# A two-block network in one program: the routing's order and the places of weights and tokens in SBUF

## The chip, the cores and the metric

One core of a Trainium2 chip runs the whole program. The metric is the device time of one execution in microseconds. TensorE is PE in the profile, its weight loads PEld, VectorE is DVE, ScalarE is ACT, GpSimd is POOL, and SP issues most of the transfers from memory.

## The reference

All is float32, for 256 tokens of 1024 features, one batch. Shortened:

```python
# first block
h = rms_norm(x, norm1_g);  proj = h @ w_in
y = gates[0] * conformer_conv(...) + gates[1] * mla(...)      # 31-tap conv; attention with 8 heads
x = x + y @ w_out
x = x + (silu(conv3(h2 @ w_up)[gate]) * conv3(h2 @ w_up)[up]) @ w_down      # D_FF = 2816
x = rms_norm(x, norm_f_g)
# second block
x = x + pool_conv_mixer(rmsnorm(x))
x = x + swiglu(rmsnorm(x), gate, up, down)                    # D_FF = 2816
x = x + sliding_window_attention(rmsnorm(x)) @ w_o + b_o      # 16 heads, 2 of keys
h = rmsnorm(x, od_norm_ffn)
top_vals, top_idx = top_k(h @ w_router, 2)                    # 8 experts
x = x + sum(combine[e] * ((silu(h @ w_gate[e]) * (h @ w_up[e])) @ w_down[e]))   # 1024 x 3584 each
return rmsnorm(x, final_norm)
```

## The kernel before

**The dense stage.** Everything ahead of the experts keeps the tokens as columns: a tile holds two blocks of 128 features by 256 tokens ("pair", 2048 bytes in each of 128 partitions). For accuracy each weight chunk and each token tile is split into two parts in the format fp32r, a high and a low one: ACT copies the chunk's high part (`whi`), DVE subtracts it (`wlo`). `mm3` multiplies high by high, high by low and low by high: three products of 256 columns, each with a weight load of 128 x 128. Token tiles have names such as xnh/xnl (normed tokens), hh/hl (hidden), xqh/xql, oh/ol. Weights arrive as chunks of up to 1 MB (`raw`); SP issues them in the order of use, as far ahead as there are buffers.

**The routing** stands at the end of `odd`, in the last of four steps over the attention's output projection. Its rows' names are: `gw` the router's weights, `lg`/`l` the logits, `acc` and `sq` the sums of squares for the norm, `rs` its reciprocal root, `sel` the selection of two experts, `place` a token's place in its expert, `S` the matrix that gathers tokens, `xe` the gathered tokens. Steps marked `high_priority` are ordered by a scheduler that may move instructions on each engine; inside `manual_schedule` an engine's instructions stand as written. Before the change the SP queue stands as written throughout, and PE from the experts on.

**The experts.** `gate`, `up` and `down_stage` stream 352 MB of expert weights. Here the weights are the moving operand and the gathered tokens (64 columns of them at a time) are loaded. Buffers for these weights are taken over from pools that the dense stage gives up (`more0` to `more6`, and `extra0` to `extra2` where whi and wlo were).

**Where tiles lie.** Pools are laid out one after another from the low end of SBUF (`cp`, `rawp`, `sm`, `pp`, `bp`, ...), those with `side="right"` from the high end (`whip`, `wlop`, later `extra`, `ep`, `xp`). In the built program, counted from the last multiple of 512 bytes, the buffers of `rawp` start at 384, those of `pp` and `bp` (token tiles) at 128, those of whi and wlo at 480, the `more` pools at 128.

**Warm-up products** are products of constants that nobody reads: `warm(n)` makes n of 128 x 128 x 128; `warm_forms` makes some at the program's start, while the first transfers are under way. The last lines of the dense step and of the warm-up are:

```python
self.mm(ps[:, f], hi[:, cs], xh, first and k == 0 and f == 0, False)
self.mm(ps[:, f], hi[:, cs], xl, False, False)
self.mm(ps[:, f], lo[:, cs], xh, False, last and k == kn - 1)
```

A plain fp32 product has two records of each kind in the trace, an fp32r product one.

Of the kernel before, what the change touches and what calls it, by code (L numbers as in the profile page):

```python
# [34 lines left out]
NSIDE = 32  # L35
NCAP = NMAIN + NSIDE
LCAP = 128
WARM = (25, 8, 0)
FIRST_PARTS = 4
ORDER = (0, 1, 3, 4, 2, 5, 6)  # L40
N_BRIEF = 22
# [18 lines left out]
N_MM = 5  # L60
N_RAW = 6
N_PAIR = 22

# [306 lines left out]
class Body:  # L370
# [61 lines left out]
    def warm_forms(self):  # L432

        nc = self.nc
        c = self.pair("const", F32, (128, 512))
        nc.vector.memset(c, 1.0)
        self.warm(8)
        banks = [self.bank((128, 512)) for _ in range(2)]
        for n in range(2):
            self.mm(banks[n // 2 % 2][64 * (n % 2):64 * (n % 2) + 64], c[:, 64 * (n % 2):64 * (n % 2) + 64], c, True, True)  # L440
        for n in range(8):
            q = slice(32 * (n % 4), 32 * (n % 4) + 32)
            self.mm(banks[n // 4 % 2][q], c[:, q], c, True, True)

    def next(self, kn):
        self.w = self.st.next(kn)
# [92 lines left out]
    def body(self):  # L539
        tc, nc, ctx, a = self.tc, self.nc, self.ctx, self.a  # L540
        pool = lambda n, b, **kw: ctx.enter_context(tc.tile_pool(name=n, bufs=b, **kw))
        self.cp = pool("cp", 1)
        self.raw = pool("rawp", N_RAW)
        self.split = ExitStack()
        self.whi, self.wlo = (self.split.enter_context(tc.tile_pool(name=n, bufs=b, side="right"))
                              for n, b in (("whip", N_HI), ("wlop", N_LO)))
        self.sm, self.pp = pool("sm", 8), pool("pp", N_PAIR)
# [79 lines left out]

    def block1(self):
        nc = self.nc
        u = self.wp.tile([128, 4, 286], F32, name="wide")  # L630
# [17 lines left out]
        lat, lp, sq = self.act("lat", 6), self.parts("lat", 6), self.act("lsq", 6)  # L648
        kr, t = self.pair("kr"), self.pair("krt")
# [371 lines left out]
    def odd(self):  # L1021
# [38 lines left out]
        with self.tc.issue_after(self.last_sink.ins):  # L1060
# [2 lines left out]
        self.bp = None  # L1063
        self.rp = self.ctx.enter_context(self.tc.tile_pool(name="rows", bufs=N_ROW, reuse_waits="tile"))
        self.brief = ExitStack()
        more = [self.brief.enter_context(self.tc.tile_pool(name=f"more{i}", bufs=1, reuse_waits="tile"))
                for i in range(len(ORDER))]
        self.st.ring = deque([more[i] for i in ORDER] + [self.raw] * N_RAW)
# [5 lines left out]
                                self.iota[:, :NE, None].to_broadcast([128, NE, NE]), op=ALU.is_lt)  # L1074
        lg = self.aux((128, 2, 8))
        self.ex, self.S = {}, {}
        for j in range(4):
            ps = self.dense(o)
            with self.tc.high_priority(offset=HASTE):
                x = self.x.p[j]  # L1080
                for f in range(2):
                    nc.vector.scalar_tensor_tensor(x[:, f], ps[:, f], self.par("od_b_o_2", 2 * j + f), x[:, f],
                                                   op0=ALU.add, op1=ALU.add)
                for f in range(2):
                    for b in range(2):
                        self.mm(lg[:, b], x[:, f, 128 * b:128 * b + 128], gw[:, 2 * j + f], j + f + b == 0, j + f == 4)
                ps = self.aux()
                for f in range(2):
                    for b in range(2):
                        nc.tensor.transpose(ps[:, b, 128 * f:128 * f + 128], x[:, f, 128 * b:128 * b + 128], self.ident)  # L1090
                self.stat_add(s, x)
                if j == 3:
                    self.rms(s)
                    place = self.rank(lg)
                cs = slice(256 * (j % 2), 256 * (j % 2) + 256)
                for b in range(2):
                    nc.scalar.activation(self.x0[b][j // 2][:, cs], ps[:, b], AF.Copy)
                if j == 3:
                    place()
                    self.first_feats()  # L1100
        self.dbg("x5", self.x)
        self.counts()
        self.split.close()
# [7 lines left out]
        self.normal()  # L1111
        self.weigh()
        self.weights(0, self.slots((0,))[:, :, 0])

    def attend(self, i, kv, V, o):

# [40 lines left out]
    def rank(self, lg):  # L1157
# [12 lines left out]
        nc.vector.tensor_scalar(sel, rank, 2.0, None, op0=ALU.is_lt)  # L1170
        self.warm(WARM[1])
        pc = self.aux((128, 3, NE))
        self.mm(pc[:, 0], self.upper, sel[:, 0], True, True)
        self.mm(pc[:, 1], self.upper, sel[:, 1], True, False)
        self.mm(pc[:, 1], self.ones, sel[:, 0], False, True)
        for b in range(2):
            self.mm(pc[:, 2], self.ones, sel[:, b], b == 0, b == 1)
        self.warm(WARM[2])
        self.place = sm("place")

        def place():
            nc.vector.scalar_tensor_tensor(self.place, pc[:, :2], 1.0, sel, op0=ALU.add, op1=ALU.mult)
            self.tally = self.cp.tile([128, NE], F32, name="tally")
            self.tally_i = self.cp.tile([128, NE], I32, name="tallyi")
            nc.vector.tensor_copy(self.tally, pc[:, 2])
            nc.vector.tensor_copy(self.tally_i, self.tally)

        return place

    def rms(self, s):  # L1190

        nc = self.nc
        ps = self.aux((128, 2, 2))
        for b in range(2):
            for f in range(2):
                self.mm(ps[:, b], s["acc"][:, f, 128 * b:128 * b + 128], self.ones[:, :2], f == 0, f == 1)
        self.rs = self.cp.tile([128, 2], F32, name="rs")
        nc.scalar.activation(self.rs, ps[:, :, 0], AF.Sqrt, scale=1.0 / D, bias=self.eps)
        nc.vector.reciprocal(self.rs, self.rs)
# [43 lines left out]
    def first_feats(self):  # L1243

        nc = self.nc
        S = self.pair("S0", shape=(128, 2, NCAP))
        for b in range(2):
            nc.vector.tensor_scalar(S[:, b], self.iota[:, :NCAP], self.place[:, b, 0:1], self.rs[:, b:b + 1],
                                    op0=ALU.is_equal, op1=ALU.mult)
        xe = [self.pair("xe", shape=(128, 4, NCAP)) for _ in range(2)]  # L1250
        for h in range(2):
            ps = self.aux((128, 4, NCAP))
# [370 lines left out]
```

## Time and profile before

| what | us |
|---|---|
| median of 3 runs (lowest, highest) | 1610.0 (1608.72, 1610.36) |
| the profiled execution: its time | 1611.13 |
| the profiled execution: span from first to last instruction | 1609.1 |
| TensorE busy | 1557.9 |
| DVE busy | 645.5 |
| ACT busy | 476.3 |

The span is that of one execution taken by the hardware profiler. A product's start is observed and its end is modelled, so neighbouring products overlap in the records, and the distance from start to start is what tells their pace. The granted clock of TensorE is 1.00 at 2.4 GHz and 0.50 at 1.2 GHz.

### The profile page before, as it was taken

What the parts mean: (1) busy time and instruction counts of PE and PEld (TensorE: products, weight loads), DVE (VectorE), ACT (ScalarE), POOL (GpSimd) and SP (SyncE); (2) the same over time, 40 slices, a digit from 0 to 9 for tenths busy, and PEclk for the clock granted to TensorE, in tenths of its full rate; (3) what the DMA queues carried; (4) which work ended last, traced back from release to release, by engine and by line L of the source; (5) the groups of instructions that cost most, each with busy time, mean ns of one, the idle gap of its engine ahead of it and who ended that gap; (6) DMA issues with size and microseconds to landing.
All of it is one profiled execution on the core that took longest, in us unless ns stands there. A gap on an engine that the chain in (4) does not pass through costs nothing. (4 is left out here: it accounts for less than half of the span.)

```text
span 1609.1 us, 25856 instructions
## 1 busy us (share of the span) xinstructions
PE 1557.9 (97%) x11090; PEld 1031.0 (64%) x11090; DVE 645.5 (40%) x1138; ACT 476.3 (30%) x800; POOL 14.1 (1%) x41
## 2 busy tenths in 40 slices
PE   9999999999999999998999999999999999999885
PEld 8989999999999999997333433334333333433221
DVE  6795889866866665663100202102011011020111
ACT  6536566555454444662000100001000000001001
POOL 0000000000000110000000000000000000000000
PEclk9999999999999999998999999999999999999999
DMA  9334445455955655443899999999999999999996
GB/s 338 113 128 157 184 178 190 165 180 215 193 227 183 213 196 198 150 184 161 307 366 421 415 421 419 419 420 418 420 420 418 421 413 387 420 389 421 419 418 257
DMA packets 73337, 481.09 MB, mean 299 GB/s; under 512 B 8208, under 2 KB 8224, under 8 KB 29296
## 3 DMA queue, kind: packets, MB, share of 16 engines
q1 hardware_dynamic: 71136, 472.42, 73.8%
q0 software_dynamic: 1632, 5.89, 2.2%
q8 instruction: 105, 1.72, 0.4%
q10 hardware_dynamic: 432, 0.80, 0.1%
q14 instruction: 32, 0.26, 0.0%
HBM read 474.89 MB, written 4.19 MB: 298 GB/s over the span
## 5 line engine op out<-in xcount | busy, mean ns | idle before, releaser
L423 PE MATMUL mm<-raw,xe 128*64 128x512 f32 (+3 forms) x3072 | 508.1, 543 | 14.8 <-DMA raw<-w_exp 10.2
L423 PEld LDWEIGHTS mm<-raw,xe 128*64 128x64 f32 (+1 forms) x3072 | 174.3, 127 | 326.3 <-issue 269.5
L339 DVE TENSOR_TENSOR wlo<-raw,whi 128x1024 fp32r<-128x1024 f32 x210 | 248.7, 1195 | 73.9 <-ACT whi L335 73.5
L335 ACT ACTIVATE whi<-raw 128x1024 fp32r<-128x1024 f32 x210 | 212.0, 1032 | 203.5 <-issue 122.5
L423 PE MATMUL mm<-xnh,whi 128*128 128x256 f32 x912 | 257.1, 282 | 0.0
L423 PE MATMUL mm<-xnh,wlo 128*128 128x256 f32 x912 | 256.0, 281 | 0.0
L423 PE MATMUL mm<-xnl,whi 128*128 128x256 f32 x912 | 255.9, 281 | 0.0
L423 PE MATMUL mm<-raw,ht 128*64 128x512 f32 x896 | 202.7, 597 | 13.2 <-DMA raw<-w_exp 10.2
L423 PEld LDWEIGHTS mm<-xnh,whi 128*128 128x128 f32 x912 | 171.8, 188 | 0.7 <-issue 0.6
L423 PEld LDWEIGHTS mm<-xnl,whi 128*128 128x128 f32 x912 | 171.8, 188 | 0.1
L423 PEld LDWEIGHTS mm<-xnh,wlo 128*128 128x128 f32 x912 | 171.8, 188 | 0.0
L423 PEld LDWEIGHTS mm<-raw,ht 128*64 128x64 f32 x896 | 63.7, 136 | 142.9 <-issue 108.4
L423 PE MATMUL mm<-hh,wlo 128*128 128x256 f32 x352 | 98.7, 280 | 0.0
L423 PE MATMUL mm<-hl,whi 128*128 128x256 f32 x352 | 98.7, 280 | 0.0
L423 PE MATMUL mm<-hh,whi 128*128 128x256 f32 x352 | 98.7, 280 | 0.0
L1348 ACT ACTIVATE ht<-aux 128x512 f32<-128x512 f32 (+1 forms) x32 | 15.7, 541 | 255.4 <-PE aux L1346 255.4
L1291 DVE MEMSET mm<- 128x512 f32 (+2 forms) x40 | 16.0, 400 | 186.0 <-ACT h L1333 183.6
L1338 DVE TENSOR_TENSOR h<-mm,h 128x512 f32<-128x512 f32 (+1 forms) x48 | 28.4, 619 | 145.8 <-PE mm L423 144.7
L1437 ACT ACTIVATE of<-mm 64x512 f32<-64x512 f32 x16 | 9.5, 593 | 241.0 <-PE mm L423 200.1
L1360 DVE COPY hts<-aux 128x512 f32<-128x512 f32 (+1 forms) x16 | 10.0, 624 | 174.2 <-PE aux L1358 103.8
L423 PEld LDWEIGHTS mm<-hl,whi 128*128 128x128 f32 x352 | 66.3, 188 | 0.0
L423 PEld LDWEIGHTS mm<-hh,whi 128*128 128x128 f32 x352 | 66.3, 188 | 0.0
(332 smaller groups left out, 1796.6 us busy)
## 6 DMA issues: line engine op xcount, KB each, us to landing
raw<-w_exp SPq DMA_DIRECT2D x239, 1024.0 KB, 19.1
raw<-w_dense SPq DMA_DIRECT2D x104, 1024.0 KB, 4.8
raw<-w_exp SPq DMA_DIRECT2D x128, 768.0 KB, 15.0
raw<-w_dense SPq DMA_DIRECT2D x10, 768.0 KB, 4.4
skew<-band POOLq DMA_DIRECT2D x1, 3072.0 KB, 36.4
bias<-skew POOLq DMA_DIRECT2D x8, 256.0 KB, 3.1
x<-x_t SPq DMA_DIRECT2D x4, 256.0 KB, 5.5
raw<-w_dense SPq DMA_DIRECT2D x4, 256.0 KB, 6.4
```

The lines of the kernel that those rows point to most:

```text
L335: nc.scalar.activation(self.hi[:, cut], t[:, cut], AF.Copy)
L339: nc.vector.tensor_sub(self.lo[:, cut], t[:, cut], self.hi[:, cut].bitcast(F32))
L423: self.nc.tensor.matmul(out, a, b, start=start, stop=stop, skip_group_check=True)
L1291: self.nc.vector.memset(ps, 0.0)
L1338: self.nc.vector.tensor_mul(h[t], u, h[t])
L1348: nc.scalar.activation(t[:, :c], ps[:, :c], AF.Copy)
L1360: return turn, lambda: nc.vector.tensor_copy(t[:, :c], ps[:, :c])
L1437: nc.scalar.activation(o[:NMAIN], main[64 * c:64 * c + 64], AF.Copy)
```

## The change

Four things change together.

1. The routing's last step is written out in `odd` under `manual_schedule` for PE, DVE and ACT: three warm-up products first, then the router's products, the transposes, the statistic, the selection, the placement and the first gather. The eight warm-up products between statistic and selection are gone. The copies of the expert counts (`tally`) follow the gather matrix.
2. The norm's statistic multiplies with the full 128 columns of `ones`, where it took 2, and takes `sq` of the last step as a second operand, where DVE had added it to `acc`.
3. Unused tiles ("pad") and one widened tile move the pools: raw, whi, wlo, `more`, `extra`, `ep` and `xp` then start at multiples of 512 bytes, `pp` and `bp` at 192 past one.
4. `warm_forms` makes 36 fp32r products of 256 columns, with the moving operand at four places (528, 560, 592 and 608 bytes past the loaded one), in place of ten fp32 products of 64 and 32 rows.

```diff
-WARM = (25, 8, 0)
+WARM = (3,)
+PAD_CP = 32
+PAD_SM = 8
+PAD_PAIR = 48
+PAD_RIGHT = 120
+PAD_MORE = 80
...
-        banks = [self.bank((128, 512)) for _ in range(2)]
-        for n in range(2):
-            self.mm(banks[n // 2 % 2][64 * (n % 2):64 * (n % 2) + 64], c[:, 64 * (n % 2):64 * (n % 2) + 64], c, True, True)
-        for n in range(8):
-            q = slice(32 * (n % 4), 32 * (n % 4) + 32)
-            self.mm(banks[n // 4 % 2][q], c[:, q], c, True, True)
+        r, ps = self.pair("constr", F32R, (128, 512)), self.bank()
+        nc.vector.tensor_copy(r, c)
+        for b in (132, 140, 148, 152):
+            for _ in range(9):
+                self.mm(ps[:, 0], r[:, :128], r[:, b:b + 256], True, True)
...
+        self.cp.tile([128, PAD_CP], F32, name="pad")
+        pool("padr", 1, side="right").tile([128, PAD_RIGHT], F32, name="pad")
...
+        with self.tc.manual_schedule(engines=every):
+            self.warm(WARM[0])
+            self.rest(3, ps)
+            self.logit(3, lg, gw)
+            sq = self.pair("sq")
+            nc.scalar.activation(sq, self.x.p[3], AF.Square)
+            ps = self.turned(3)
+            self.turned_out(3, ps)
+            place, tally = self.rank(lg, lambda: self.rms((s["acc"], sq)))
+            place()
+            self.first_feats(tally)
...
-        self.warm(WARM[1])
+        beside()
...
-        ps = self.aux((128, 2, 2))
+        ps = self.aux((128, 2, 128))
         for b in range(2):
-            for f in range(2):
-                self.mm(ps[:, b], s["acc"][:, f, 128 * b:128 * b + 128], self.ones[:, :2], f == 0, f == 1)
+            for i, t in enumerate(tiles):
+                for f in range(2):
+                    self.mm(ps[:, b], t[:, f, 128 * b:128 * b + 128], self.ones, i + f == 0, i + f == 2)
```

The helpers `rest` (bias and residual), `logit`, `turned` (transposes) and `turned_out` hold the lines that stood in the loop.

TensorE's order in the last routing step, before the change, from the router's products (`gw`) to the first expert products (`raw,xe`); of the sixteen gather products one row stands:

```order
L423 MATMUL aux<-gw,x 128x8 x2
L1090 MATMUL aux<-squares,x 128x128 x2
L423 MATMUL aux<-gw,x 128x8 x2
L1090 MATMUL aux<-squares,x 128x128 x2
L423 MATMUL aux<-ones,acc 128x2 x4
L423 MATMUL aux<-ones 128x128 x8
L423 MATMUL aux<-sel,squares 128x8 x2
L423 MATMUL aux<-sel,ones 128x8 x3
L423 MATMUL aux<-S_8180,x_7844 128x96
...
L423 MATMUL mm<-raw,xe 64x512 x3
```

The same place after the change:

```order
L428 MATMUL aux<-ones 128x128 x3
L428 MATMUL aux<-gw,x 128x8 x4
L1138 MATMUL aux<-squares,x 128x128 x4
L428 MATMUL aux<-ones,acc 128x128 x2
L428 MATMUL aux<-ones,sq 128x128 x2
L428 MATMUL aux<-ones,acc 128x128 x2
L428 MATMUL aux<-ones,sq 128x128 x2
L428 MATMUL aux<-sel,squares 128x8 x2
L428 MATMUL aux<-sel,ones 128x8 x3
L428 MATMUL aux<-S_8219,x_7885 128x96
...
L428 MATMUL mm<-raw,xe 64x512 x3
L1315 MATMUL aux<-squares,S 96x128 x2
```

Three warm-up products stand ahead of the router's and none behind the statistic, and the statistic has eight products. After the three expert products and the two transposes of `S` come 13 more expert products before TensorE reads the counts, as before the change.

DVE's order at the same place, before:

```order
L1165 COPY l<-aux 128x16
L1166 TENSOR_TENSOR c<-l 128x16x8
L1167 TENSOR_TENSOR c<-l 128x16x8
L493 TENSOR_TENSOR acc<-acc,sq 128x512
L1168 TENSOR_TENSOR c<-c,low 128x16x8
L1169 TENSOR_REDUCE rank<-c 128x16
L1199 RECIPROCAL rs<-rs 128x2
L1170 TENSOR_SCALAR sel<-rank 128x16
```

And after:

```order
L1196 COPY l<-aux 128x16
L1197 TENSOR_TENSOR c<-l 128x16x8
L1198 TENSOR_TENSOR c<-l 128x16x8
L1199 TENSOR_TENSOR c<-c,low 128x16x8
L1200 TENSOR_REDUCE rank<-c 128x16
L1201 TENSOR_SCALAR sel<-rank 128x16
...
L1232 RECIPROCAL rs<-rs 128x2
```

The add of the squares is gone, and the selection stands ahead of the reciprocal, with seven small operations for the tops between them. At the program's start TensorE has, after the change:

```order
L428 MATMUL aux<-ones 128x128 x8
L428 MATMUL mm<-constr 128x256 x36
L428 MATMUL mm<-xg,raw 128x256 x7
L428 MATMUL aux<-ones,acc 128x2 x4
L428 MATMUL mm<-xg,raw 128x256 x2
```

Before, ten products of `const` stood for the 36, and ten of `xg,raw` ahead of the statistic.

## Rows read from the trace of the kernel before

**Rows 1.** The page, busy time of each engine (share of the span) xinstructions.

```profile
PE 1557.9 (97%) x11090; PEld 1031.0 (64%) x11090; DVE 645.5 (40%) x1138; ACT 476.3 (30%) x800; POOL 14.1 (1%) x41
```

**Rows 2.** Busy time by stretch; last come granted clock, DMA share, GB/s.

```profile
743.00:764.00 21.00, 18.57 (x92) 11.72 (x95) 7.15 (x28) 2.58 (x4) 0.00 (x0) 0.78 0.03 13
...
850.00:1140.00 290.00, 285.22 (x1882) 112.53 (x1878) 40.96 (x81) 24.77 (x49) 0.00 (x0) 1.00 1.01 419
```

**Rows 3.** Groups by line, 8 to 735 us: xcount, busy us, mean ns, idle.

```profile
L423 PE MATMUL mm<-xnh,whi 128*128 128x256 f32 x912 | 257.1, 282 | 0.0
...
L423 PE MATMUL mm<-convh,whi 128*128 128x256 f32 x32 | 8.6, 286 | 0.0
```

**Rows 4.** TensorE in order of time, first feed-forward layer: start us, length.

```profile
299.99 0.28 PE L423 MATMUL mm<-xnh,whi 128*128 128x256 f32 x1
...
303.90 0.28 PE L423 MATMUL mm<-xnh,whi 128*128 128x256 f32 x1
```

**Rows 5.** The same view, second feed-forward layer.

```profile
499.81 0.28 PE L423 MATMUL mm<-xnh,whi 128*128 128x256 f32 x1
...
503.68 0.28 PE L423 MATMUL mm<-xnh,whi 128*128 128x256 f32 x1
```

**Rows 6.** The same view, query projection.

```profile
661.38 0.28 PE L423 MATMUL mm<-xqh,whi 128*128 128x256 f32 x1
...
662.83 0.28 PE L423 MATMUL mm<-xqh,whi 128*128 128x256 f32 x1
```

**Rows 7.** The same view, a later gather of two experts' tokens, 192 columns.

```profile
967.37 0.27 PE L423 MATMUL aux<-S,xnh 128*128 128x192 f32 x1
...
970.60 0.27 PE L423 MATMUL aux<-S,xnl 128*128 128x192 f32 x1
```

**Rows 8.** The same view, products of 512 columns in the first block.

```profile
69.86 0.40 PE L423 MATMUL mm<-wlo,lath 128*128 128x512 f32 x1
...
71.27 0.39 PE L423 MATMUL mm<-wlo,lath 128*128 128x512 f32 x1
```

**Rows 9.** In order of time, routing; in brackets idle time before and releaser.

```profile
734.73 0.87 DVE L1082 SCALAR_TENSOR_TENSOR x<-mm,vecs,x 128x256 f32<-128x256 f32 x2 [4.61 <-PE mm L423]
...
736.35 0.41 PE L1090 MATMUL aux<-squares,x 128*128 128x128 f32 x2
...
737.98 1.39 PE L423 MATMUL aux<-ones,acc 128*128 128x2 f32 x8 [1.22 <-DVE acc L493]
...
739.23 3.76 PE L423 MATMUL aux<-ones 128*128 128x128 f32 x16
...
739.70 0.17 DVE L1199 RECIPROCAL rs<-rs 128x2 f32<-128x2 f32 x1 [1.21 <-ACT rs L1198]
739.78 0.15 DVE L1170 TENSOR_SCALAR sel<-rank 128x16 f32<-128x16 f32 x1
...
743.50 1.43 PE L423 MATMUL aux<-sel,ones 128*128 128x8 f32 x6
744.96 0.17 DVE L1182 SCALAR_TENSOR_TENSOR place<-aux,sel 128x16 f32<-128x16 f32 x1 [3.73 <-PE aux L423]
...
745.65 6.87 PE L423 MATMUL aux<-S,x 128*128 128x96 f32 x32 [0.72 <-DVE tallyi L1186]
...
752.45 1.93 PE L423 MATMUL mm<-raw,xe 128*64 128x512 f32 x6
...
763.70 0.33 SPq L317 DMA_DIRECT2D raw<-w_exp  x1
```

**Rows 10.** Busy time by stretch, routing; granted clock stands third from the end.

```profile
738.40:738.60 0.20, 0.20 (x4) 0.20 (x3) 0.09 (x1) 0.00 (x0) 0.00 (x0) 0.69 0.97 410
...
739.00:740.00 1.00, 1.00 (x5) 1.00 (x6) 0.30 (x4) 0.57 (x2) 0.00 (x0) 0.50 0.97 410
```

**Rows 11.** In order of time, the program's start, TensorE.

```profile
4.72 2.93 PE L423 MATMUL mm<-const 128*64 128x512 f32 x20
...
8.95 4.55 PE L423 MATMUL mm<-xg,raw 128*128 128x256 f32 x20 [1.30 <-DMA raw<-w_dense]
```

More of the change, by code (lines that the diff above doesn't have):

```diff
@@ L546, in body @@
                               for n, b in (("whip", N_HI), ("wlop", N_LO)))
-        self.sm, self.pp = pool("sm", 8), pool("pp", N_PAIR)
+        self.sm = pool("sm", 8)
+        self.sm.tile([128, PAD_SM], F32, name="pad")
+        pool("padp", 1).tile([128, PAD_PAIR], F32, name="pad")
+        self.pp = pool("pp", N_PAIR)
         self.brief, self.ep = ExitStack(), None
@@ L629, in block1 @@
         nc = self.nc
-        u = self.wp.tile([128, 4, 286], F32, name="wide")
+        u = self.wp.tile([128, 4, 288], F32, name="wide")[:, :, :286]
         self.wide = u
@@ L1065, in odd @@
         self.brief = ExitStack()
+        self.ctx.enter_context(self.tc.tile_pool(name="padm", bufs=1)).tile([128, PAD_MORE], F32, name="pad")
         more = [self.brief.enter_context(self.tc.tile_pool(name=f"more{i}", bufs=1, reuse_waits="tile"))
@@ L1076, in odd @@
         self.ex, self.S = {}, {}
+        every = {getattr(mybir.EngineType, n) for n in ("PE", "DVE", "Activation")}
         for j in range(4):
             ps = self.dense(o)
+            if j == 3:
+                break
             with self.tc.high_priority(offset=HASTE):
-                x = self.x.p[j]
-                for f in range(2):
[L1082 to L1100, printed above, removed]
+                self.rest(j, ps)
+                self.logit(j, lg, gw)
+                ps = self.turned(j)
+                self.stat_add(s, self.x.p[j])
+                self.turned_out(j, ps)
+        with self.tc.manual_schedule(engines=every):
[9 more added lines that the diff above has]
+            self.first_feats(tally)
         self.dbg("x5", self.x)
@@ L1113, in odd, with rest, logit, turned @@
         self.weights(0, self.slots((0,))[:, :, 0])
+    def rest(self, j, ps):
+        x = self.x.p[j]
+        for f in range(2):
+            self.nc.vector.scalar_tensor_tensor(x[:, f], ps[:, f], self.par("od_b_o_2", 2 * j + f), x[:, f],
+                                                op0=ALU.add, op1=ALU.add)
+    def logit(self, j, lg, gw):
+        for f in range(2):
+            for b in range(2):
+                self.mm(lg[:, b], self.x.p[j][:, f, 128 * b:128 * b + 128], gw[:, 2 * j + f], j + f + b == 0, j + f == 4)
+    def turned(self, j):
+        ps = self.aux()
+        for f in range(2):
+            for b in range(2):
+                self.nc.tensor.transpose(ps[:, b, 128 * f:128 * f + 128], self.x.p[j][:, f, 128 * b:128 * b + 128], self.ident)
+        return ps
+    def turned_out(self, j, ps):
+        cs = slice(256 * (j % 2), 256 * (j % 2) + 256)
+        for b in range(2):
+            self.nc.scalar.activation(self.x0[b][j // 2][:, cs], ps[:, b], AF.Copy)
     def attend(self, i, kv, V, o):
@@ L1155, in attend, with rank @@
         self.turn_out(o, i, po, turned, m[:, 8:12])
-    def rank(self, lg):
+    def rank(self, lg, beside):
         nc = self.nc
@@ L1177, in rank @@
             self.mm(pc[:, 2], self.ones, sel[:, b], b == 0, b == 1)
-        self.warm(WARM[2])
         self.place = sm("place")
@@ L1184, in place, with tally, rms @@
             self.tally_i = self.cp.tile([128, NE], I32, name="tallyi")
+        def tally():
             nc.vector.tensor_copy(self.tally, pc[:, 2])
             nc.vector.tensor_copy(self.tally_i, self.tally)
-        return place
-    def rms(self, s):
+        return place, tally
+    def rms(self, tiles):
         nc = self.nc
-        ps = self.aux((128, 2, 2))
+        ps = self.aux((128, 2, 128))
         for b in range(2):
-            for f in range(2):
-                self.mm(ps[:, b], s["acc"][:, f, 128 * b:128 * b + 128], self.ones[:, :2], f == 0, f == 1)
+            for i, t in enumerate(tiles):
+                for f in range(2):
+                    self.mm(ps[:, b], t[:, f, 128 * b:128 * b + 128], self.ones, i + f == 0, i + f == 2)
         self.rs = self.cp.tile([128, 2], F32, name="rs")
@@ L1241, in gains, with first_feats @@
         return self.par("od_norm_ffn_2", 4 * h + k, n)[:, :, None].to_broadcast([128, n, width])
-    def first_feats(self):
+    def first_feats(self, tally):
         nc = self.nc
@@ L1249, in first_feats @@
                                     op0=ALU.is_equal, op1=ALU.mult)
+        tally()
         xe = [self.pair("xe", shape=(128, 4, NCAP)) for _ in range(2)]
```

## The prediction

> **What bounds the kernel now.** I read the page first, then the busy time by stretches, then single products in order of time. TensorE is busy for 97% of the span [rows 1]. That share hides two stages. After about 764 us the eight experts run, and from 850 us the transfers of expert weights are saturated: the 16 DMA engines show a share of 1.01 and 419 GB/s [rows 2]. So the end comes when the last weight has landed, and that stream has one long hole: from 743 to 764 us it moves 13 GB/s [rows 2], because every buffer is full; the queue's next transfer is issued at 763.70 [rows 9], after the first expert has used some. If that expert starts earlier by some time, the hole closes and the end moves by the same time. All that lies ahead of the expert is therefore worth one for one: the dense stage and the routing.
>
> **The dense stage** (about 24 to 735 us) is a chain of products, each with its own weight load. They come in eight groups of three, from 912 down to 32 instructions each [rows 3], together 3 x (912 + 352 + 96 + 80 + 64 + 64 + 32 + 32) = 4,896 products. In the first feed-forward layer 33 steps take 303.90 - 299.99 = 3.91 us, 118.5 ns each [rows 4]. In the second the same 33 steps take 3.87 us, 117.3 ns [rows 5]. In the query projection 12 steps take 1.45 us, 120.8 ns [rows 6]. No engine is waited for there, the instructions have one shape, and tokens and weights keep one distance in memory; so the spacing has several levels that the kernel's code does not choose. I take 117.9 ns, the middle of the two long stretches. A nanosecond on every product is 4.9 us.
>
> **Routing** runs from 734.73 (DVE gets the last dense tile) to 752.45 us, when the first expert product starts: 17.7 us [rows 9]. The statistic's products wait for DVE's add and start at 737.98; sixteen records of warm-up then stand from 739.23 to 742.99, though the selection that they hold up is ready at 739.78 + 0.15 [rows 9]. Between 738.4 and 738.6 us the granted clock falls, to 0.50 [rows 10], the lower of the two levels, 1.2 GHz, after TensorE had almost nothing to do from 736.8 to 738.0. All that follows is paid at that level: the gather has 32 records in 6.87 us, 215 ns each [rows 9].
>
> **The change, part by part.**
>
> *Routing in written order.* Three warm-up products go ahead of the router's, into the time in which TensorE waits for DVE (734.7 to 735.3), eight behind them go. The logits no longer alternate with the transposes. The order on DVE loses the add of the squares and the selection is no longer behind the reciprocal. The worked sequence, if the clock stays at 2.4 GHz: router and transposes end at 736.8 as now (736.35 + 0.41) [rows 9], nothing being added to them. The statistic reads the accumulated tile and the last squares apart, eight products with 128 columns instead of four with 2: 16 records. Their price at the higher clock does not stand in routing; the nearest row is the later gather, with the same size of weight load, 29 steps in 970.60 - 967.37 = 3.23 us, 111.4 ns [rows 7]. 16 x 111.4 = 1.8 us, to 738.6. By then the selection is ready: of what stands ahead of it now, the reciprocal's wait of 1.2 us [rows 9] and the add of the squares go. Ten selection records, 1.1 us: 739.7. Placement and the two slot tiles took 745.65 - 744.96 = 0.7 us [rows 9]: 740.5 with a latency. 32 gather records at 111.4: 3.6 us, 744.1. Against 752.45 that is **-8.3 us**. What stands behind on DVE (the tally's copies, moved behind the slots) is needed only after 16 expert products. The wait of the St transposes for DVE just after the first three expert products stays, since DVE's order there is the same. If the clock falls all the same, the records cost 215 ns: 16 + 10 + 32 of them take 12.5 us and the start comes at 750.0, **-2.4 us**. I take -8.1: with longer products of the statistic and without that idle stretch, the case is nearer to the dense stretch ahead, which holds the higher level.
>
> *Wide ones* add 8 records, 0.9 us, counted above; they replace a 1.2 us wait for DVE.
>
> *Other warm-up products* at the start: today 2.93 us of them from 4.72, then a wait for the first weights until 8.95 [rows 11]. 36 products at 118.5 ns take 4.3 us, to 9.0: the cover is the 1.3 us wait, and it is used up. The order puts the first statistic behind 7 products instead of 10, which can leave a short wait for DVE's squares. **+0.3 us**, between 0 and +1.
>
> *The addresses.* Today tokens start 128 and split weights 480 bytes past a multiple of 512, a distance of 160; then 192 and 0, a distance of 192. No instruction is added. No row has the new distance, so the price is bounded. Best: the loads alone. Products of 192 columns or fewer leave the load as the limit, and stand at 111.4 ns [rows 7]: -6.5 ns, -32 us. Worst seen: all at the 120.8 of the query stretch [rows 6]: +2.9 ns, +14 us. In the gather of [rows 7] both operands start at multiples of 64 bytes, as they will in the dense stage, whereas weights at 480 do not; but its streams are shorter. I therefore go half-way between that row and the best dense one, (111.4 + 117.3) / 2 = 114.4: 3.5 x 4.9 = **-17 us**.
>
> [...]
>
> The expert products have no loss to win back: there the transfers set the pace.
>
> **Sum** against the profiled execution, 1611.1 us (span 1609.1 and 2.0 around it): 1611.1 - 8.1 + 0.3 - 17 = 1586.3. The median of the runs is 1.1 lower: **1585 us**.
>
> **Rivals.**
>
> *Distance without effect.* For it: products with 512 columns, one load each, take 6 steps in 71.27 - 69.86 = 1.41 us, 235 ns [rows 8], twice 117.5. A loss that came from the load should not double with the columns; one that the moving operand makes by itself would, and would not care where the weights lie. Against it: the several levels. Then 1611.1 - 8.1 + 0.3 - 1.1 = **1602 us**.
>
> *Clock falls anyway.* The 0.9 us between selection and gather, or the short logits, may be enough. Then 5.7 us come back: 1591 with the gain in the dense stage, 1608 without it.
>
> *Slower.* The new distance puts both streams where they meet more often, and all 4,896 products stand at the level of [rows 6] or over it. From 117.9 + 7.8 / 4.9 = 119.5 ns the routing's gain is used up; at 120.8 the time is 1602 + 14 = **1616 us**. Against it: that level is the one seen least.
>
> **Chances.** Spacing falls by over a nanosecond 0.60, stays 0.28, rises by over a nanosecond 0.12; the clock holds 0.7 in each. Forecast (spacing falls, clock holds) 0.42; spacing falls with the clock lost 0.18; no effect 0.28; slower stretch 0.12. 0.2% is 3.2 us, about what this kernel's measurement can tell from no change. Faster: all of the 0.60, 0.7 x 0.28 = 0.20 of "stays", together 0.80. Same (1607 to 1613): the rest of "stays", 0.08, and a little of "rises", 0.10. Slower 0.10. Range: 1566 (the bound at 111.4 gives 1570) to 1607; outside lie some 0.05 below and 0.15 above. The forecast's own range, with falls of 1.5 to 6.5 ns, is 1570 to 1595.
>
> **What would show it.** The 33 steps in each feed-forward layer: 3.8 us means right, 3.9 means no effect, 3.68 the bound. The first expert product some 9.4 us after DVE's last dense tile, with the clock at 1.00 throughout; 15 us would mean that the clock fell. The hole in the transfers shrinks by 8 us. The prediction is wrong if the spacing keeps its levels, if it goes over 119.5, or if the experts' transfers do not start sooner although the first product does.

## The result and the profile after

The changed kernel takes 1581.6 us (median of 4 runs, 1580.65 to 1583.09) against 1610.2 us before; the ratio is 0.9824, with a 95% interval of 0.9807 to 0.9841. The forecast was 1585 us, range 1566 to 1607. The profiled execution took 1583.09 us, its span fell from 1609.1 to 1581.0 us, by 28.1. Four marks cut it into the terms of the prediction's sum: the first statistic (13.35 us before), DVE's last dense tile and the first expert product [rows 9], and the end.

| term | forecast, us | measured, us | from |
|---|---|---|---|
| start | +0.3 | +4.0 | 13.35 to 17.39 |
| dense stage | -17 | -18.9 | tile at 734.73, now 719.82, less the start |
| routing | -8.1 | -6.8 | 17.72, now 10.95 |
| experts | 0 | -6.4 | the rest of 28.1 |

So the total came within 4 us with two errors of 4 and 6 us in it that lay in opposite directions: that closeness is in part luck.

The dense products, TensorE in order of time, the changed kernel: the first and the last of 34 in the first feed-forward layer, and of 34 in the second (these answer to [rows 4, 5]).

```profile
299.84 0.28 PE L428 MATMUL mm<-xnh,wlo 128*128 128x256 f32 x1
...
303.58 0.28 PE L428 MATMUL mm<-xnh,wlo 128*128 128x256 f32 x1
...
499.83 0.28 PE L428 MATMUL mm<-xnh,wlo 128*128 128x256 f32 x1
...
503.57 0.28 PE L428 MATMUL mm<-xnh,wlo 128*128 128x256 f32 x1
```

Both times 33 steps take 3.74 us, 113.3 ns, where they took 3.91 and 3.87. Over all unbroken steps of the stage (some 4,760) the mean went from 118.2 to 113.8 ns.

Routing in order of time, answering to [rows 9]:

```profile
719.82 0.88 DVE L1126 SCALAR_TENSOR_TENSOR x<-mm,vecs,x 128x256 f32<-128x256 f32 x2 [4.39 <-PE mm L428]
...
721.74 0.61 PE L428 MATMUL aux<-ones,acc 128*128 128x128 f32 x4
...
722.85 0.17 DVE L1201 TENSOR_SCALAR sel<-rank 128x16 f32<-128x16 f32 x1
...
723.53 0.51 PE L428 MATMUL aux<-sel,squares 128*128 128x8 f32 x4
723.89 0.81 PE L428 MATMUL aux<-sel,ones 128*128 128x8 f32 x6
725.43 5.41 PE L428 MATMUL aux<-S,x 128*128 128x96 f32 x32 [0.72 <-DVE S L1281]
...
730.77 1.93 PE L428 MATMUL mm<-raw,xe 128*64 128x512 f32 x6
```

The statistic starts without a wait, its 16 records take 723.53 - 721.74 = 1.8 us, and the selection is ready before they end. Only the gather is longer than forecast, 730.77 - 725.43 = 5.3 us for 3.6. The granted clock (third from the end) shows why:

```profile
724.00:726.00 2.00, 1.28 (x12) 1.22 (x12) 1.41 (x12) 1.98 (x3) 0.00 (x0) 1.00 1.01 418
726.00:728.00 2.00, 2.00 (x15) 2.00 (x15) 0.42 (x4) 1.96 (x4) 0.00 (x0) 0.70 1.01 426
728.00:730.00 2.00, 2.00 (x11) 2.00 (x11) 0.92 (x5) 0.00 (x0) 0.00 (x0) 0.50 0.48 201
```

It fell to 0.50, the lower of the two levels, during the gather, whose first product had waited 0.72 us for DVE; 16 of the gather's 31 steps stand at 213 ns instead of 111. The trace has the clock as a share alone; the 1.2 and 2.4 GHz given with it are an estimate at one column a cycle: at the lower pace 256 columns take 213 ns (the start, below), at least 1.2 a ns, and 1.00 is twice that.

The start, TensorE's first statistic before the change, then TensorE and DVE after it (answers to [rows 11]):

```profile
13.35 0.95 PE L423 MATMUL aux<-ones,acc 128*128 128x2 f32 x8
```

```profile
1.07 3.78 PE L428 MATMUL aux<-ones 128*128 128x128 f32 x16 [1.07 <-DVE eps L582]
...
6.63 0.23 DVE L614 CAST identr<-squares 128x128 fp32r<-128x128 f32 x1 [5.07 <-DMA squares<-squares]
6.77 0.42 DVE L444 CAST constr<-const 128x512 fp32r<-128x512 f32 x1
...
7.25 7.28 PE L428 MATMUL mm<-constr 128*128 128x256 f32 x36 [2.40 <-DVE constr L444]
...
14.37 3.18 PE L428 MATMUL mm<-xg,raw 128*128 128x256 f32 x14
17.39 0.95 PE L428 MATMUL aux<-ones,acc 128*128 128x2 f32 x8
```

The 36 products do not start at 4.7 but at 7.25 us: their constants are copied on DVE behind a copy that waits 5.07 us for a transfer. They take 7.1 us, not 4.3.

The transfers from 900 to 1300 and from 1300 to 1500 us, before and after (last: DMA share, GB/s):

```profile
900.00:1300.00 400.00, 392.20 (x2546) 149.89 (x2546) 53.23 (x103) 31.35 (x62) 0.00 (x0) 1.00 1.01 419
1300.00:1500.00 200.00, 196.85 (x1299) 77.93 (x1291) 26.68 (x52) 17.06 (x34) 0.00 (x0) 1.00 0.99 406
```

```profile
900.00:1300.00 400.00, 395.68 (x2606) 151.28 (x2604) 51.78 (x98) 31.61 (x62) 0.00 (x0) 1.00 1.01 425
1300.00:1500.00 200.00, 192.73 (x1215) 76.09 (x1213) 26.72 (x53) 17.06 (x34) 0.00 (x0) 1.00 0.98 406
```

At the same busy share of the engines they move 425 GB/s instead of 419 in the first stretch. In the second both move 406, so the gain is not one of the whole stage.

### The profile page after: what moved, and what is told of

Same layout as the page of the kernel before. It is cut to its first block, busy times and chain, and to the rows that moved or that the text cites. A ratio compares the mean times of both kernels' runs of the same rounds, so it can differ in the third digit from the quotient of the medians.

```text
span 1581.0 us, 25883 instructions
## 1 busy us (share of the span) xinstructions
PE 1534.3 (97%) x11104; PEld 1014.0 (64%) x11104; DVE 644.0 (41%) x1138; ACT 476.5 (30%) x800; POOL 14.1 (1%) x41
## 5 line engine op out<-in xcount | busy, mean ns | idle before, releaser
L428 PE MATMUL mm<-xnh,whi 128*128 128x256 f32 x912 | 253.4, 278 | 0.0
L428 PE MATMUL mm<-xnh,wlo 128*128 128x256 f32 x912 | 252.2, 277 | 0.0
L428 PE MATMUL mm<-xnl,whi 128*128 128x256 f32 x912 | 252.1, 276 | 0.0
```

What stands on the lines that cost most here:

```text
L428: self.nc.tensor.matmul(out, a, b, start=start, stop=stop, skip_group_check=True)
```

## The experiments

Times are medians; the kernel before ran beside each (1609 to 1611 us).

**e1_places**: the kernel before with the third part of the change alone (the pads and the widened tile).

> The kernel before with the third part of the change alone: raw, weights and experts' buffers at multiples of 512 bytes, tokens 192 past one. My theory (the places set the pace of the dense products, and the pace at which transfers fill the buffers): the dense products step at 113.8 ns instead of 118.2, TensorE's last dense tile comes 18.7 us sooner, routing stays at 17.7 us, the transfers after 850 us move 425 GB/s instead of 419 and give 6.4 us more: about 1585 us. Rival (the 6.4 us behind the first expert come from the new routing or the buffers' other times, not from the places): 419 GB/s stay and the time is about 1591 us.

Measured: 1590.5 us, not the 1585 of the theory; the runs were 1590.1, 1592.4, 1591.0 and 1580.7. The transfers move 425 GB/s from 900 to 1300 us, so that rate comes with the places, and from the first expert product to the end it takes 849.9 us, with the old routing, where the kernel before took 856.6. But the dense stage gained less than in the changed kernel: its mean step is 115.4 ns. Same view as above, first and second layer:

```profile
299.79 0.28 PE L428 MATMUL mm<-xnh,wlo 128*128 128x256 f32 x1
...
303.68 0.28 PE L428 MATMUL mm<-xnh,wlo 128*128 128x256 f32 x1
...
499.82 0.28 PE L428 MATMUL mm<-xnl,whi 128*128 128x256 f32 x1
...
503.56 0.28 PE L428 MATMUL mm<-xnl,whi 128*128 128x256 f32 x1
```

33 steps take 3.89 us in the first layer, 117.9 ns, and 3.74 in the second. With the same addresses there are two levels. Some 1,600 products at 4.4 ns more are 7.0 us; what the other 3 us between its runs are isn't shown, since one of them has a profile. The recorded mean clock points at the old routing: 0.996 in the run of 1580.7 against 0.994 in the profiled one. An estimate from these two: 2 to 3 us less lost to the lower clock.

**e2_tokens160**: the token pools 32 bytes lower.

```diff
-PAD_PAIR = 48
-PAD_MORE = 80
+PAD_PAIR = 40
+PAD_MORE = 88
```

> The changed kernel with the token pools 160 bytes past a multiple of 512 instead of 192; all else stays, weights at 0. Distance theory: 160 is the distance of the kernel before, so the dense products go back to 118 ns and the time is about 1582 + 19 = 1601 us. Rival (what counts is that the weights start at a multiple of 512, wherever the tokens are): 113.8 ns stay, 1582 us.

Measured: 1598.9 us, mean step 118.1 ns, with the weights still at multiples of 512. So it isn't the weights' place by itself; whether it is the tokens' own place or the distance, e6_curve tells. That it gave 1599 and not 1601 is for the most part the routing: in this run the clock held, and the first expert product came 9.33 us after DVE's last tile instead of 10.95.

**e3_raw384**: raw and the `more` pools 384 past a multiple of 512.

```diff
-        self.cp.tile([128, PAD_CP], F32, name="pad")
-PAD_PAIR = 48
-PAD_MORE = 80
+PAD_PAIR = 80
+PAD_MORE = 48
```

> The changed kernel with the buffers raw and more0 to more6 moved 384 bytes past a multiple of 512; split weights, tokens and extra0 to extra2 stay. Theory (transfers fill buffers at multiples of 512 faster): the dense stage and the routing are unchanged, after 850 us the transfers fall back to about 420 GB/s, and the time is 5 to 6 us over the changed kernel's, about 1587 us. Rival (the higher rate comes from elsewhere, such as tokens and expert products out of the way): 425 GB/s stay, 1582 us.

Measured: 1586.4 us (1585.8 to 1586.8), 4.8 over the changed kernel; dense mean 114.2 ns. From the first expert product to the end the profiled run takes 854.8 us, 4.6 more than the changed kernel. The transfers:

```profile
900.00:1300.00 400.00, 393.63 (x2592) 150.72 (x2588) 49.70 (x95) 31.61 (x62) 0.00 (x0) 1.00 1.01 421
```

In this kernel all but `extra0` to `extra2` are back off the multiple of 512, and most of the higher rate is gone too. So in these kernels the rate went with the buffers' places: 425 GB/s with all of them at multiples of 512, 421 with the three, 419 with none.

**e6_curve**: 64 groups of products from one constant tile, their distance varied.

```diff
+        for a, step in ((0, 4), (32, 8), (120, 8)):
+            for d in range(0, 128, step):
+                self.mm(self.aux((128, 128)), self.ones, self.ones, True, True)
+                for _ in range(24):
+                    self.mm(ps[:, 0], r[:, a:a + 128], r[:, a + d:a + d + 256], True, True)
```

> The changed kernel with 64 groups of 24 products of 256 columns in fp32r added to its warm-up, all from one constant tile: the loaded operand 0, 128 or 480 bytes past the tile's start (itself 192 past a multiple of 512) and the moving one at distances of 0 to 508 bytes, in steps of 16 bytes for the first and 32 for the others. One product with ones stands ahead of each group. Distance theory: the pace is a function of the distance alone, the same from all three starts, about 118 ns at 160 and about 114 at 192. Rival (alignment of each operand by itself): the pace follows the start of the loaded operand, and not the distance. If neither, all groups stand at one pace. Some 180 us longer in all.

TensorE in order of time, the groups at 160, 176 and 192 bytes (loaded operand at 0), then those at 160 and 192 with the loaded operand at 480:

```profile
45.06 3.06 PE L428 MATMUL mm<-constr 128*128 128x256 f32 x24
47.96 0.38 PE L428 MATMUL aux<-ones 128*128 128x128 f32 x2
48.10 3.10 PE L428 MATMUL mm<-constr 128*128 128x256 f32 x24
51.03 0.38 PE L428 MATMUL aux<-ones 128*128 128x128 f32 x2
51.17 3.00 PE L428 MATMUL mm<-constr 128*128 128x256 f32 x24
54.01 0.38 PE L428 MATMUL aux<-ones 128*128 128x128 f32 x2
...
176.34 3.09 PE L428 MATMUL mm<-constr 128*128 128x256 f32 x24
179.27 0.38 PE L428 MATMUL aux<-ones 128*128 128x128 f32 x2
179.41 2.98 PE L428 MATMUL mm<-constr 128*128 128x256 f32 x24
182.24 0.38 PE L428 MATMUL aux<-ones 128*128 128x128 f32 x2
```

From a group's start to the ones behind it: 2.90, 2.93 and 2.84 us; 2.93 and 2.83 with the other start. Mean step behind the second, ns, loaded operand at 0, worked out from the single records:

```
distance   0    16    32    48    64    80    96   112   128   144   160   176   192   208   224   240
ns     119.5 118.8 116.7 118.3 117.9 120.2 119.6 115.4 118.6 118.7 117.4 119.2 114.2 118.8 118.1 117.4
```

Distances of 256 to 496 repeat this within 0.1 ns, and the other two starts stay within 1.3 ns of it (160: 117.4 and 118.6; 192: 113.4 and 113.5). So in these chains the pace goes by the distance modulo 256, whatever the start of the three, and of the steps of 16 bytes 192 is the best. Each figure is one chain of 24; that a distance can have a second level shows at 160 here, and at 192 in the next run.

**e8_fine**: steps of 4 bytes around the two dips, and sixteen chains at 192.

```diff
+        for d in [*range(25, 32), *range(45, 52)]:
+            self.mm(self.aux((128, 128)), self.ones, self.ones, True, True)
+            for _ in range(24):
+                self.mm(ps[:, 0], r[:, :128], r[:, d:d + 256], True, True)
+        for n in range(16):
+            for _ in range(4):
+                self.mm(self.aux((128, 2)), self.ones, self.ones[:, :2], True, True)
+            for _ in range(24):
+                self.mm(ps[:, 0], r[:, :128], r[:, 48:304], True, True)
```

> The changed kernel with two sets of products added to its warm-up: 24 products each at distances of 100 to 124 and 180 to 204 bytes in steps of 4, and then 16 times 24 products at a distance of 192 behind four products of 2 columns. Theory of a narrow dip: 113 to 114 ns only at 192 and 115 to 116 at 112, over 117 elsewhere; rival: the dip is broad, or its floor of 111.4 ns lies between the steps of 16 bytes. Theory of a drawn level: of the 16 chains at 192 some stand at 113.4 and some at 117.8 ns, and each keeps its level to its end; rival: all stand at 113.4, and the second level needs something else of the dense stage.

Measured: the dips are single points, 113.5 at 192 between 120.0 at 188 and 119.9 at 196, and 114.3 at 112 between 119.6 and 121.8. The slowest chain is near the second dip: 128.5 at 104. At 204 it is 116.6, a little under the theory's 117. Of the sixteen chains (the built order put one product of each ahead of the last break, so 23 stand together) the first stands at 113.3 and the fifteen others at 117.8 ns. The first two:

```profile
58.83 2.87 PE L428 MATMUL mm<-constr 128*128 128x256 f32 x23
61.53 0.72 PE L428 MATMUL aux<-ones 128*128 128x2 f32 x6
...
62.46 2.96 PE L428 MATMUL mm<-constr 128*128 128x256 f32 x23
65.26 0.72 PE L428 MATMUL aux<-ones 128*128 128x2 f32 x6
```

2.70 and 2.80 us from the same 23 products, with the same operands. The second level exists outside the dense stage, and each chain keeps its own.

**e4_cast**: the copy of the constants on ACT, fewer products.

```diff
-        nc.vector.tensor_copy(r, c)
+        nc.scalar.activation(r, c, AF.Copy)
-            for _ in range(9):
+            for _ in range(6):
```

> The changed kernel with the copy of the warm-up's constants made by ACT, which is idle then, instead of DVE, where it stands behind a copy that waits for a transfer until 6.6 us, and with 24 of those products instead of 36. My theory (the pause of 2.4 us from 4.85 to 7.25 us keeps TensorE at the lower clock, and 29 of the 36 products are paid at 213 ns): the products follow the first warm-up without a pause, the pace changes from 213 to about 118 ns by 7.5 us, the first product of the program proper starts at about 9 us instead of 14.4, the first statistic 4 to 5 us sooner, and the time is about 1577 us. Rival (the clock rises at its own time, 13.4 us, whatever stands before): 24 products at 213 ns, the first product at 10 us, the following at full rate only from 13.4 us, and 1579 to 1580 us.

Measured: 1577.4 us (1576.4, 1577.3, 1577.5 and once 1583.9), ratio to before 0.9815 (0.9788 to 0.9842).

```profile
4.50 3.10 PE L428 MATMUL mm<-constr 128*128 128x256 f32 x24
9.04 3.69 PE L428 MATMUL mm<-xg,raw 128*128 128x256 f32 x16 [1.45 <-ACT xg L604]
12.77 1.05 PE L428 MATMUL aux<-ones,acc 128*128 128x2 f32 x8
```

Without the pause the products run at about 118 ns from 4.7 us on; the statistic comes 4.6 us sooner than in the changed kernel, and DVE gets the last dense tile 4.3 us sooner. The rival falls. But the pause alone does not hold the lower level, for e3_raw384 has the same pause:

```profile
7.25 4.50 PE L428 MATMUL mm<-constr 128*128 128x256 f32 x36 [2.40 <-DVE constr L444]
...
14.61 0.95 PE L428 MATMUL aux<-ones,acc 128*128 128x2 f32 x8
```

There one of the 35 steps is over 200 ns, and the statistic comes at 14.61 us instead of 17.39. In the other six profiles with the pause 21 to 28 steps are; in the five without it (e4_cast, e7_all, e9_wide, e11_kick, e12_best) 1 to 12 of 23. So the pause makes a late rise of the clock likely and not certain; what decides is open.

**e5_fill**: three products ahead of the gather.

```diff
             self.mm(pc[:, 2], self.ones, sel[:, b], b == 0, b == 1)
+        self.warm(3)
```

> The changed kernel with three more warm-up products between the selection's products and the first gather, where TensorE waits 0.72 us for DVE. My theory (that wait, right behind ten short records, is what brings the clock down in the gather): the gather's 32 records all step at 111 ns, 3.6 us instead of 5.3, and the time is 1.7 us shorter, 1579.9 us. Rival (the short products of 8 columns before it are enough, or the fall comes from further back): the clock falls again at 726.5 to 727 us, 5.3 us stay, 1581.6 us or 0.1 over.

Measured: 1588.1 us (1580.7, and three of 1587.7 to 1588.6), so slower; but not in the routing:

```profile
731.66 0.91 PE L428 MATMUL aux<-ones 128*128 128x128 f32 x6
732.52 3.78 PE L428 MATMUL aux<-S,x 128*128 128x96 f32 x32
736.24 1.93 PE L428 MATMUL mm<-raw,xe 128*64 128x512 f32 x6
```

The gather takes 3.7 us, and the first expert product comes 9.32 us after the last tile. The loss is in the first feed-forward layer, which stands at 117.8 ns as in e1_places. One profile doesn't settle what the fill does, since the clock held without it too in e2_tokens160, e4_cast and e6_curve. Over all profiles: without the fill it fell in five (the changed kernel, e3_raw384, e8_fine, e10_breaks, e12_best) and held in three; with it, it held in all four.

**e7_all**: both, and the first expert's S ahead of the low parts.

```diff
+        S = self.slots((0,))
         self.normal()
         self.weigh()
-        self.weights(0, self.slots((0,))[:, :, 0])
+        self.weights(0, S[:, :, 0])
```

> The changed kernel with both of these (the copy on ACT with 24 products, the three warm-up products ahead of the gather) and with the matrix S of the first expert's tokens made ahead of the low parts of the normed tokens on DVE, so that the transposes of S do not wait 1.71 to 2.3 us behind the first expert products. If the three gains add up: 4.5 + 1.7 + 2.0 us, about 1573 us. Rival (the experts' transfers set the end, and the sooner start is lost where TensorE waits for them): 1577 us or more.

Measured: 1581.8 us, in six runs 1575.7, 1575.9, 1581.8, 1581.8, 1589.0 and 1589.1. So the 1573 us of the three gains added up did not come. The steps of 6 to 7 us between the runs are the size of one long chain at the higher level. In the profiled run (1581.8) the first layer stands at 117.8 ns and the second at 113.4. From DVE's last dense tile to the end it takes 857.3 us, e5_fill 858.7: S ahead of the low parts gave some 1.5 us of the 2 expected.

**e9_wide**: the dense stage's statistics with 128 columns of ones.

```diff
-        ps = self.aux((128, 2, 2))
+        ps = self.aux((128, 2, 128))
-                self.mm(ps[:, b], t[:, 128 * b:128 * b + 128], self.ones[:, :2], i == 0, i == len(tiles) - 1)
+                self.mm(ps[:, b], t[:, 128 * b:128 * b + 128], self.ones, i == 0, i == len(tiles) - 1)
```

> The kernel of e7_all with the statistics of the dense stage multiplied by all 128 columns of ones where they take 2, so that the long chain of the first feed-forward layer starts behind products of 128 columns. Drawn-level theory (at a distance of 192 a chain holds 113.4 or 117.8 ns from its start on, and what stands just ahead decides; behind products of 2 columns it was 117.8 in 15 of 16 chains, behind 128 columns 113.4): the first layer's products step at 113.4 ns in every run, the runs do not spread over 13 us as those of e7_all did, and the median is 1574 to 1576 us. Rival (the level is drawn anew in each run by something else): the runs spread from 1575 to 1589 us again, median near 1582.

Measured: 1582.8 us, in six runs 1575.8, 1576.2, three of 1582.8 to 1583.1, and 1589.3. The rival holds: the width of the products ahead of a chain doesn't decide its level. In this profile the first layer has the low level and the second the high one.

**e10_breaks**: thirty chains at 192 behind breaks of five widths.

```diff
+        for z in (2, 8, 32, 64, 128):
+            for k in (1, 4):
+                for _ in range(3):
+                    self.brk(z, k)
+                    for _ in range(24):
+                        self.mm(ps[:, 0], r[:, :128], r[:, 48:304], True, True)
```

Here `brk` makes k products of ones with z columns.

> The changed kernel with 30 chains of 24 products at a distance of 192 added to its warm-up: three each behind one or four products with ones of 2, 8, 32, 64 and 128 columns. Drawn-level theory: each kind of break gives one level, 113.4 or 117.8 ns, in all or nearly all of its three chains, the low one behind 128 columns and the high one behind 2. Rival (chance): both levels behind every kind.

Measured: all thirty at 113.3 to 114.2 ns, those behind 2 columns too. Neither expectation holds. The breaks of four products of 2 columns differ from those of e8_fine in the tiles that they write and in the one product of the chain that stood inside them there; whether either counts no run tells.

**e11_kick**: e7_all with single products of ones inside both long chains (the line below in the first layer, its like in the second).

```diff
+                self.warm(i in (1, 2) and part == 0)
                 p = self.dense(self.xn)
```

> The kernel of e7_all with one product of ones (128 columns, two records) set into the long chain of each feed-forward layer at two places, some 100 and 200 products behind the chain's start. Theory (the level is drawn at each break of the chain, and a break by one such product has given the low one in all 40 or so chains measured at 192): both layers stand at 113.4 ns behind the second of them in every run, the runs no longer spread over 13 us, and the median is 1576 to 1578 us, some 1 us of it for the four products. Rival (an entire execution has its level, drawn before): the long chains of some runs stay at 117.8 ns in spite of the breaks, and the runs lie at 1576, 1583 and 1590 us as those of e7_all and e9_wide did.

Measured: 1589.5 us, four runs of 1588.1 to 1590.8. TensorE around the first such product of the second layer:

```profile
466.19 0.28 PE L428 MATMUL mm<-xnh,wlo 128*128 128x256 f32 x1
...
467.21 0.28 PE L428 MATMUL mm<-xnh,wlo 128*128 128x256 f32 x1
467.32 0.39 PE L428 MATMUL aux<-ones 128*128 128x128 f32 x2
467.46 0.36 PE L428 MATMUL mm<-xnh,whi 128*128 128x256 f32 x1
467.67 0.28 PE L428 MATMUL mm<-xnl,whi 128*128 128x256 f32 x1
...
468.73 0.28 PE L428 MATMUL mm<-xnl,whi 128*128 128x256 f32 x1
```

Nine steps take 1.02 us ahead of it, 113 ns, and 1.06 behind it, 118 ns. In the first layer the first such product turned 117.8 into 113.6, and the second one turned it back. So a break can change the level within a run, and the chain holds it until the next; but it doesn't always give the low one. Neither expectation holds: behind the second product both layers of the profiled run stand at 117.8 ns, and the four runs lie near the highest step of e7_all, not on three.

**e12_best**: e4_cast with the S ahead of the low parts.

> The kernel of e4_cast (constants copied by ACT, 24 products) with the matrix S of the first expert's tokens made ahead of the low parts on DVE, and without the three products ahead of the gather. The wait behind the first expert products falls from 2.3 us to under 1 us, which is worth some 1.5 us one for one: the runs in which both feed-forward layers stand at 113.4 ns come at 1575 to 1576 us, those with one of them at 117.8 some 6.8 us later, with both 13.6 us later. Theory (the level is drawn in each run at the breaks of the chain): the runs fall on these three steps and not between them. Rival (e4_cast's three runs of four at the low level were no chance but come from its start): all runs at 1575 to 1576 us. On the clock in the gather: if it falls in some runs' profile without the three products, 5.3 us stand there, else 3.7.

Measured: 1583.9 us, five runs of 1578.7, 1581.6, 1583.9, 1584.1 and 1585.3. TensorE's wait for S is 0.92 us, under 1 as expected, where e4_cast has 1.71; it now stands ahead of the first expert products. The profiled run (1578.7) has both layers low, but the clock fell in the gather, and once more in the experts:

```profile
1374.00:1378.00 4.00, 4.00 (x12) 1.25 (x13) 0.36 (x1) 0.00 (x0) 0.00 (x0) 0.57 1.01 428
```

The granted clock reads 0.57 there though TensorE was busy throughout, in the 4 us ahead too. Product by product, the run loses 1.7 us against e4_cast there, and not in waits for the transfers. The runs don't lie on the three steps alone, so neither expectation holds as it stands. Of the versions tried e4_cast is the fastest by its median, 4 us under the changed kernel, though the intervals against the kernel before overlap.

## Why the prediction was right, and where it was not

**The dense stage.** That the distance sets the pace was right, and the term some 10% small: 114.4 ns was chosen half-way between two rows, and 113.8 was measured. The reason given for a gain, that both operands then start at multiples of 64 bytes, was wrong. In e6_curve they do so at distances of 0, 64 and 128 too (the tile itself starts at 192), which stand at 119.5, 117.9 and 118.6 ns; and 192 gives 113.5 with the loaded operand at 480, where they don't. Nothing else in the prediction singled 192 out, and that it is the best of the steps measured was luck. The bound from the gather with 192 columns (111.4) isn't reached at any of the distances measured. That the load sets this bound was the author's estimate; what the changed kernel's trace shows is that the columns don't: with a load of 128 x 128 each, the median step from record to record is 110 to 112 ns for products of 2, 8, 64, 96, 128 and 192 columns. e2_tokens160 and e6_curve show that the distance does it. The several levels of [rows 4 to 6], which the prediction set against the rival "distance without effect", are two kinds of thing: the distance sets which levels there are (113.4 and 117.8 at 192; 117.3 and 118.7 at 160, by the stretches of e2_tokens160), and a break of the chain can change from one to another. The 120.8 ns of [rows 6], at the same distance of 160, fits neither of its two and stays open.

**The rival "distance without effect"** had the products of 512 columns for it, whose loss doubled with the columns. The conclusion from it, that the weights' place can't matter, was wrong: in the changed kernel nine such steps take 75.40 - 73.33 = 2.07 us, 230 ns instead of 235, so their pace moved with the places too. Nor is the pace free of the distance at 256 columns: 113.5 ns at 192 and 120.0 at 188 from the same tile with nothing else changed. Why a distance modulo 256 should count stays open; no run looks inside.

**The rival "slower"**, all products at 120.8 ns, did not come (that two streams meet more often was a guess, which no run shows), but its like did on a smaller scale: e1_places, e5_fill and e11_kick have the new distance and one or both layers at 117.8. The four runs of the changed kernel lie within 2.5 us, so no long chain of theirs seems to have been high; e1_places has the same addresses and was 10 us over its best in three runs of four. Another set of runs of the changed kernel might hold some at 1588.

**Routing.** The worked sequence gave 9.4 us from DVE's last tile, with the clock held; it is 9.33 in every run where it held without further edits. In the profiled run it fell, not by the 5.7 us of the rival "clock falls anyway" but by 1.6, because only the gather's later half was hit. The step that failed is the sentence that the case is nearer to the dense stretch: it looked at the statistic. The rival had named the place, the wait between selection and gather, 0.9 us there and 0.72 as measured. The chance of 0.7 for the clock to hold was high: of the eight profiles without the fill it held in three.

**The start** is the step that was wrong, +4.0 for +0.3. The sum let the products follow on the first warm-up as the old ones did; it did not look at what is queued ahead of the new copy on DVE. And it priced them at the dense stage's 118.5 ns, though behind that pause 27 of their 35 steps stood at 213 in this run (one in e3_raw384, where the start cost +1.3 in place of +4.0). The late start is 2.5 us, the lower level 2.8, together 14.37 for 9.0 at the first product of the program; 1.4 us come back because 7 products and not 10 stand ahead of the statistic, a line that the prediction counted as a possible loss.

**The experts.** That the end moves by the same time as the first expert product holds: in five kernels with the places of the changed one (it, e1_places, e2_tokens160, e4_cast, e5_fill) that product starts between 724.9 and 748.3 us, and the rest takes 849.4 to 850.5. The hole in the transfers shrank by the 8 us that were forecast: it lay from 743.6 to 764.7 us before, and lies from 730.1 to 743.0 after. What moved besides is the rest itself, 856.6 us before. In e3_raw384, where most of the buffers are off the multiples again, the end comes 1.8 us beyond the sooner start, against 6.4 here. The 4.6 us between them are what the prediction lacked: it moved the buffers of the weights and priced only the products that read them, not the transfers that fill them. Measured, 419 GB/s is 1.4% under 425. Why the place of a buffer counts stays open.

## What to carry to other kernels

When a chain of products with a load each stands some nanoseconds over the pace of products with fewer columns (118 over 111 ns here), vary the distance between the two operands in SBUF before looking for a lost instruction: it cost nothing, and was worth 19 us of 1610. When a pool moves, price every engine that touches it, the transfers too (425 GB/s for 419 here). When an edit adds an operation that something waits for, read what stands ahead of it in its engine's order: one copy at the wrong place cost 4 us, and 10 lines of the order would have told.

## What the runs showed of the hardware that was not expected

- The pace of 256-column fp32r products with a load each depends on the distance from the loaded to the moving operand modulo 256 bytes: 113.4 to 114.2 ns at 192, 114.3 to 115.4 at 112, and 116.7 to 120.2 at the other steps of 16 (e6_curve, e8_fine). The slowest seen is 128.5 at 104 (e8_fine).
- At one distance there is a second level (at 192, 117.8 ns beside 113.4, in e8_fine and in the dense stage of e1_places). A chain held its level without a break for 184 us (e5_fill, first layer), and one other product between can turn it either way (e11_kick, 117.8 to 113.6 and back). What decides was not found: by e9_wide and e10_breaks not the width of the product ahead.
- At the changed kernel's start the granted clock reads 1.00 from 7 us on while the records stand 213 ns apart, as at the lower level. The trace's first record of the clock is at 13.43 us, where the steps change to some 118 ns: ahead of it that column does not tell the pace.
- With the same pause ahead of them the steps changed at 13.4 us in the changed kernel, while in e3_raw384 all but the first already stood at some 118 ns. In e12_best the granted clock reads 0.57 from 1374 to 1378 us, with TensorE busy throughout and in the 4 us ahead.
- From 900 to 1300 us the transfers moved 425 GB/s into buffers at multiples of 512 bytes (the changed kernel, e1_places), 421 with most buffers 384 past them (e3_raw384), and 419 at 128, 384 and 480 past them (the kernel before).
